# Three quads per gate/up pair, the sums of copies on VectorE, and two-bank transposes in the next pair's last chunks

## The chip, the cores and the metric

The kernel runs on one core of a Trainium2 chip. The metric is device time in microseconds (us) of one execution, as the median over repeated executions. Five engines work from their own in-order instruction streams: TensorE (PE in the profile, with its weight loads as PEld), VectorE (DVE), ScalarE (ACT), GpSimd (POOL), and SyncE (SP), which issues the weight transfers.

## The reference

Two transformer blocks over 256 positions of width 2048, all in float32. The first has three attention branches, the second a gated recurrence, a short convolution and a feed-forward network. The change lies in the feed-forward network alone:

```python
h2 = _rmsnorm(x, ffn_norm_w[l])
g, u = jnp.split(jnp.einsum('bsd,df->bsf', h2, w_gate_up[l]), 2, axis=-1)
x = x + jnp.einsum('bsf,fd->bsd', jax.nn.silu(g) * u, w_down[l])
```

Here `h2` is 256 x 2048, `w_gate_up` is 2048 x 11264 (gate and up, 5632 columns each) and `w_down` is 5632 x 2048.

## The kernel before

**Products in two parts.** A float32 product is made of three matmuls. ScalarE copies a weight tile to a rounded `wh` (`hi`, line 393), VectorE subtracts to get the rest `wl` (`lo`, line 398), and the activations are split the same way. TensorE then multiplies high by high, low by high and high by low. One matmul has 128 x 128 stationary activations and 512 moving columns of weights.

**Pieces.** All products form one list of pieces that `drive` walks through. For each piece it emits the splits of pieces up to five ahead (`feed`, with `la` = 5 and `ahead` = 1 in the feed-forward network), then the matmuls of the piece (`prod`), then what becomes due after it (`done`), and then, for most pieces, one step of the side work (`side`). What `done` and `side` emit for VectorE therefore stands in VectorE's stream behind the splits of the next five pieces. `side` moves the generators in `urgent` and `lanes`. A generator that yields n is taken up again at the n-th later step, and `wait(ev)` asks at each step whether an event was set.

**A chunk** holds two rows of 128 of the contraction for 512 columns: 12 matmuls, one load of 512 KB, one `wh` and one `wl` of 128 x 1024.

**A pair** (`Pair`, line 155) makes the 512 gate columns and the 512 up columns of block j together. For a part of the contraction it goes by quads. A quad (line 285) covers two rows of 128 of the contraction for both 512-column halves and both halves of the positions, and makes this 2 x 2 x 2 block product with seven products instead of eight (Strassen in Winograd's form), so with 21 matmuls instead of 24. In return VectorE makes four sums of weight tiles (`formt`, `formv`, lines 237 to 244) and splits four tiles: g (128 x 1024), u (128 x 512), t and v (128 x 1024 each). The seven products P1 to P7 lie in seven PSUM banks. Before, quads 0 to 3 (`NQ` = 4) cover rows 0 to 7 of the contraction, and rows 8 to 15 go by four chunks of gate (`ga`) and four of up (`gb`). The order of the pieces is quad 0, ga 0, quad 1, ga 1, quad 2, ga 2, quad 3, ga 3, gb 0 to gb 3. Jobs f1 to f10 are such pairs; f0 is made of two plain jobs.

**Sums of copies.** After the last quad ScalarE copies P1, P5, P7 and P6 to SBUF (`ps`, line 274), and the four sums of these copies follow on GpSimd (lines 276 to 282). After gb 0, `evac_a` adds P2 and P4 to two of the sums and applies silu (`sg`, lines 1875 to 1881). After the last gb, `evac_b` adds P3 and Q to the other two (`up`, line 1889) and multiplies (line 1890).

**Transposes.** The finished block j (`sg`, 256 x 512) has to be transposed and split for the down projection (`finish`, lines 1846 to 1862). From f1 on there is one PSUM bank for such side work (bank 7) and seven for products (`wide`, line 1910). `later` makes four transposes into bank 7 at the third step after the block is done, splits them (`ah` on ScalarE, `al` on VectorE) one step later, makes the other four two steps on, and splits those. For most blocks this falls among the quads of the next pair. For blocks 3, 7 and 10 a down projection follows (`fd0`, `fd1`, `fd2`), and it falls among its chunks.

**Storage.** All larger tiles share 43 slots of 128 x 1024, given out in the order in which they came free. The third pair of a group (f3, f7) can hold all 43 by the code: residual 4, `h3` 8, transposed forms 4, `ah`/`al` of three blocks 6, one `sg`, 5 raw loads, t and v, 7 `wh` and 6 `wl`.

Of the kernel before, what the change touches and what calls it, by code (L numbers as in the profile page):

```python
# [13 lines left out]
ALU = mybir.AluOpType  # L14
# [13 lines left out]
RAW = 4  # L28
LA = 3
NSLOT = 43  # L30
NQ = 4
WARM = 4
T2 = 5
RAMP = 6
# [80 lines left out]
class Chunk(Piece):  # L115
# [32 lines left out]
    def done(self, b):  # L148
        b.slots.put(self.wh, self.wl)
        if self.last:  # L150
            self.job.evac([x[:, :self.n] for x in self.job.banks])
            b.free(*self.job.banks)
# [34 lines left out]
class PairChunk(Chunk):  # L187
# [22 lines left out]
    def done(self, b):  # L210
        b.slots.put(self.wh, self.wl)
        if self.last and self.i:
            p = self.job.p
            self.job.evac_b([(p["P3"], p["C12"]), (p["Q"], p["C22"])])
            b.free(p["P3"], p["Q"])
        elif self.then:
            p = self.job.p
            self.job.evac_a([(p["P2"], p["C11"]), (p["P4"], p["C21"])])
            b.free(p["P2"], p["P4"])


class QuadPart(Piece):
# [44 lines left out]
    def done(self, b):  # L267
        b.slots.put(self.wh, self.wl)
        if self.last:
            P_ = self.pair.p  # L270
            for n in self.names:
                if n in ("P1", "P5", "P6", "P7"):
                    P_[n + "s"] = b.work([P, 512], "ps")
                    b.act(P_[n + "s"], P_[n])
                    b.free(P_[n])
            if self.kind == "v":
                p1, p5, p6, p7 = (P_[n + "s"] for n in ("P1", "P5", "P6", "P7"))
                b.tt(p6, p6, p1, ALU.add, "g")
                b.tt(p7, p7, p6, ALU.add, "g")
                b.tt(p6, p6, p5, ALU.add, "g")  # L280
                b.tt(p5, p5, p7, ALU.add, "g")
                P_.update(C11=p1, C12=p6, C21=p7, C22=p5)


def quad(pair, q, first, last):
# [12 lines left out]
class Builder:  # L298
# [1188 lines left out]
    def x_next(self, x, cb, ssp, r, store, g, name):  # L1487
# [5 lines left out]
        def later():  # L1493
            yield 2
            yield from self.gen_T(lambda t, j: x[:, t, j * P:(j + 1) * P], h, l, g=g, ev=f"{name}{cb}")
            for t in range(2):
                sq = self.work([P, 768], "sq", bufs=1)[:, :512]
                self.act(sq, x[:, t, :], AF.Square, accum_out=ssp[:, t, cb:cb + 1])
            if name == "h3" and 2 * cb < NQ:
                yield from self.gen_forms(h, l, cb)  # L1500
# [325 lines left out]
    def ffn(self):  # L1826
        nc, I, sl, jobs = self.nc, self.I, self.slots, self.jobs
        wg, wd = I["w_gate_up"][0], I["w_down"][0]
        k16 = list(range(16))
        h3 = self.h3  # L1830
        xk = lambda k: (h3[k // 4][0][:, k % 4, :], h3[k // 4][1][:, k % 4, :])
        aT, sg = {}, {}
        self.ssf = self.const([P, 2, 4], "ss_f")
        self.gf = []

        def g_evac(j):
            def evac(pts):
                if j == 0:
                    self.force("r_h3")
                s = sl.get([P, 2, 512], F32, "sg")  # L1840
                for t in range(2):
                    self.act(s[:, t, :], pts[t], AF.Silu, scale=self.r3[:, t:t + 1])
                sg[j] = s
            return evac

        def finish(j, s):
            h, l = sl.get([P, 4, 256], F32R, f"ah{j}"), sl.get([P, 4, 256], F32R, f"al{j}")
            aT[j] = (h, l)

            def later():  # L1850
                for b in range(2):
                    yield 2 if b else 3
                    p = self.ps()
                    for jj in range(2):
                        for t in range(2):
                            self.tr(p[:, jj * 256 + t * P:jj * 256 + (t + 1) * P], s[:, t, (2 * b + jj) * P:(2 * b + jj + 1) * P])
                    yield 1
                    fl = lambda a: a[:, 2 * b:2 * b + 2, :].rearrange("p a b -> p (a b)")
                    self.split(fl(h), fl(l), p)
                sl.put(s)  # L1860
                self.done(f"aT{j}")
            self.add(later(), urgent=True)
            if j == 10:
                for v in h3 + list(self.sx.values()):
                    sl.put(*v)

        def u_evac(j):
            def evac(pts):
                s = sg.pop(j)
                for t in range(2):  # L1870
                    self.stt(s[:, t, :], pts[t], self.r3[:, t:t + 1], s[:, t, :], ALU.mult, ALU.mult)
                finish(j, s)
            return evac

        def ga_evac(j):
            def evac(parts):
                s = sg[j] = sl.get([P, 2, 512], F32, "sg")
                for t, (p, q) in enumerate(parts):
                    self.tt(s[:, t, :], p, q, ALU.add)
                for t in range(2):  # L1880
                    self.act(s[:, t, :], s[:, t, :], AF.Silu, scale=self.r3[:, t:t + 1])
            return evac

        def ub_evac(j):
            def evac(parts):
                s = sg.pop(j)
                for t, (p, q) in enumerate(parts):
                    c = self.work([P, 512], "up")
                    self.tt(c, p, q, ALU.add)
                    self.stt(s[:, t, :], c, self.r3[:, t:t + 1], s[:, t, :], ALU.mult, ALU.mult)  # L1890
                finish(j, s)
            return evac

        def d_evac(third, cb):
            def evac(pts):
                x = self.x1[cb]
                if third == 2 and cb == 0:
                    for i in range(2):
                        g = sl.get([P, 1024], F32, f"gf{i}")
                        nc.gpsimd.dma_start(g, I["final_norm_w_2"][i * 1024:(i + 1) * 1024].partition_broadcast(P))  # L1900
                        self.gf.append(g)
                for t in range(2):
                    self.tt(x[:, t, :], pts[t], x[:, t, :], ALU.add)
                if third < 2 and cb == 3:
                    for v in aT.values():
                        sl.put(*v)
                    aT.clear()
            return evac

        def wide():  # L1910

            self.abanks = deque(list(range(4, 7)) + list(self.abanks))
            self.sbanks = deque([7])
            self.nraw, self.la, self.ahead = 5, 5, 1

        ak = lambda k: (aT[k // 4][0][:, k % 4, :], aT[k // 4][1][:, k % 4, :])
        xs = lambda q, i: [v[:, i, q % 2, :] for v in self.sx[q // 2]]
        for third, js in enumerate((range(4), range(4, 8), range(8, 11))):
            for j in js:
                if j == 0:  # L1920
                    jobs.append(Job(f"fg{j}", xk, wg, j * 512, 512, g_evac(j), k16, {2 * c: [f"h3{c}"] for c in range(4)}))
                    jobs.append(Job(f"fu{j}", xk, wg, 5632 + j * 512, 512, u_evac(j), k16))
                else:
                    jobs.append(Pair(f"f{j}", xk, xs, wg, j * 512, 5632 + j * 512, ga_evac(j), ub_evac(j), range(NQ), k16[2 * NQ:],
                                     wide if j == 1 else None))
            ks = list(range(4 * js[0], 4 * js[-1] + (4 if third < 2 else 4 - KG)))
            for cb in range(4):
                jobs.append(Job(f"fd{third}{cb}", ak, wd, cb * 512, 512, d_evac(third, cb), ks,
                                {2 * i: [f"aT{j}"] for i, j in enumerate(js)} if cb == 0 else None))

        for cb in range(4):
            jobs.append(Job(f"fz{cb}", ak, wd, cb * 512, 512, None, list(range(44 - KG, 44))))
# [76 lines left out]
```

## Time and profile before

| | us |
|---|---|
| median of 3 runs (2267.36 to 2269.58) | 2268.35 |
| the profiled execution | 2267.79 |
| its span | 2266.0 |
| f1 to f3, first matmul to the down projection | 141.42 |
| f4 to f7 | 179.65 |
| f8 to f10 | 132.02 |

The profiled execution took 1.8 us more than its span and is within the range of the runs. In the views, the idle time in brackets stands in front of an instruction and names what ended it; a line number is that of the kernel before, and helpers such as line 326 (`tt`) serve many callers, so that the tiles' names tell them apart. Matmuls are pipelined: one of 512 columns is shown with some 0.39 us but follows the one before it every 0.227 us, so stretches and starts are read rather than busy times.

### The profile page before, as it was taken

The page shows a single profiled execution, that of the slowest core. Times are in us where ns is not written, and L with a number is a line of the kernel's source. Part 1 is how long each engine was busy: PE and PEld are TensorE (multiplying, and loading weights), DVE is VectorE, ACT ScalarE, POOL GpSimd, SP SyncE. Part 2 cuts the span into 40 slices and gives each one's busy share as a digit, 9 for nine tenths or more (in the row PEclk, how much of TensorE's full clock was granted, in tenths as well). Part 3 has the DMA queues.
Part 4 walks back from the last instruction along what each step waited for, and adds up shares of the span by engine and source line. Part 5 has one row for each costly group of instructions (what it writes and reads, how often), then busy time and mean ns, then how long its engine had stood idle before and what let it go on. Part 6 is the DMA issues. An engine that isn't in the chain of part 4 may idle for free.

```text
span 2266.0 us, 27833 instructions
## 1 busy us (share of the span) xinstructions
PE 2220.8 (98%) x10396; PEld 1849.9 (82%) x10396; DVE 1556.0 (69%) x1774; ACT 1145.3 (51%) x1532; POOL 402.9 (18%) x284
## 2 busy tenths in 40 slices
PE   9999999999999999999999999999999999999998
PEld 7888888879888888888888888887778877788776
DVE  5675776645756654555786786566996799858984
ACT  5634545455554543353645555453554465535562
POOL 2020103102305011000473351110120011101111
PEclk9999999999999999999999999999999999999999
DMA  9556455545556565656555556554546554565572
GB/s 316 188 180 200 140 167 182 168 144 194 174 158 200 180 184 183 224 185 186 176 161 166 156 155 196 185 193 143 206 165 206 186 204 158 197 202 187 186 253 72
DMA packets 215046, 413.99 MB, mean 183 GB/s; under 512 B 13538, under 2 KB 20432, under 8 KB 214912
## 3 DMA queue, kind: packets, MB, share of 16 engines
q1 hardware_dynamic: 211968, 405.99, 55.8%
q0 software_dynamic: 2224, 5.13, 0.7%
q8 instruction: 81, 1.33, 0.2%
q10 hardware_dynamic: 720, 1.11, 0.1%
q14 instruction: 53, 0.43, 0.1%
HBM read 408.51 MB, written 3.67 MB: 182 GB/s over the span
## 4 chain that ended last, share of the span: by engine, by line
PE 78%; DVE 5%; ACT 2%; issue 1%; POOL 0%; ACTq 0%; DVEq 0%; POOLq 0%
PE acc L143 20%; PE acc L144 20%; PE acc L146 20%; PE sp L351 3%; PE acc L206 2%; PE acc L205 2%; PE acc L208 2%; PE sp L371 2%; DVE wl L398 2%; PE acc L265 2%; PE acc L263 2%; PE acc L264 2%; ACT wh L393 1%; DVE formt L326 1%; DVE formv L326 1%
## 5 line engine op out<-in xcount | busy, mean ns | idle before, releaser
L398 DVE TENSOR_TENSOR wl<-raw,wh 128x1024 fp32r<-128x1024 f32 (+2 forms) x763 | 961.8, 1297 | 319.3 <-ACT wh L393 260.6
L393 ACT ACTIVATE wh<-raw 128x1024 fp32r<-128x1024 f32 (+2 forms) x763 | 742.2, 1025 | 156.9 <-DVE wl L398 88.3
L143 PE MATMUL acc<-wh,xh 128*128 128x512 f32 (+2 forms) x864 | 339.3, 393 | 0.0
L144 PE MATMUL acc<-wh,xl 128*128 128x512 f32 (+2 forms) x864 | 335.5, 388 | 0.0
L146 PE MATMUL acc<-wl,xh 128*128 128x512 f32 (+2 forms) x864 | 229.9, 388 | 0.0
L143 PE MATMUL acc<-wh,h2h 128*128 128x512 f32 x512 | 202.2, 395 | 0.0
L144 PE MATMUL acc<-wh,h2l 128*128 128x512 f32 x512 | 199.4, 390 | 0.0
L146 PEld LDWEIGHTS acc<-wl,xh 128*128 128x128 f32 x864 | 162.2, 188 | 32.7
L144 PEld LDWEIGHTS acc<-wh,xl 128*128 128x128 f32 x864 | 162.4, 188 | 30.9
L143 PEld LDWEIGHTS acc<-wh,xh 128*128 128x128 f32 x864 | 162.4, 188 | 30.7
L326 POOL TENSOR_TENSOR ps<-ps 128x512 f32<-128x512 f32 x40 | 69.6, 1740 | 590.0 <-ACT ps L322 587.7
L143 PE MATMUL acc<-wh,ah 128*128 128x512 f32 x352 | 137.5, 391 | 0.0
L144 PE MATMUL acc<-wh,al 128*128 128x512 f32 x352 | 137.0, 389 | 0.0
L146 PE MATMUL acc<-wl,h2h 128*128 128x512 f32 x512 | 136.9, 389 | 0.0
L205 PE MATMUL acc<-wh,h3h 128*128 128x512 f32 x320 | 124.5, 389 | 0.0
L206 PE MATMUL acc<-wh,h3l 128*128 128x512 f32 x320 | 124.5, 389 | 0.0
L146 PEld LDWEIGHTS acc<-wl,h2h 128*128 128x128 f32 x512 | 96.1, 188 | 20.0
L144 PEld LDWEIGHTS acc<-wh,h2l 128*128 128x128 f32 x512 | 96.3, 188 | 18.9
L143 PEld LDWEIGHTS acc<-wh,h2h 128*128 128x128 f32 x512 | 96.2, 188 | 18.9
L393 ACT ACTIVATE wh<-formt 128x1024 fp32r<-128x1024 f32 x40 | 42.5, 1061 | 134.6 <-DVE formt L326 124.1
L146 PE MATMUL acc<-wl,ah 128*128 128x512 f32 x352 | 94.8, 389 | 0.0
L208 PE MATMUL acc<-wl,h3h 128*128 128x512 f32 x320 | 85.5, 389 | 0.0
(492 smaller groups left out, 3773.4 us busy)
## 6 DMA issues: line engine op xcount, KB each, us to landing
raw<-in_w_in_dram SPq DMA_DIRECT2D x328, 512.0 KB, 3.7
raw<-in_w_gate_up_dram SPq DMA_DIRECT2D x176, 512.0 KB, 4.6
raw<-in_w_down_dram SPq DMA_DIRECT2D x88, 512.0 KB, 4.6
raw<-in_w_out_dram SPq DMA_DIRECT2D x64, 512.0 KB, 3.8
raw<-in_w_branch_dram SPq DMA_DIRECT2D x48, 512.0 KB, 3.9
raw<-in_w_mem_kv_dram SPq DMA_DIRECT2D x31, 512.0 KB, 7.1
raw<-in_w_in_dram SPq DMA_DIRECT2D x8, 464.0 KB, 3.8
raw<-in_w_in_dram SPq DMA_DIRECT2D x8, 448.0 KB, 3.4
```

The lines of the kernel that those rows point to most:

```text
L143: b.nc.tensor.matmul(outs[t], x, self.wh[:, kk], start=self.first and kk == 0, stop=False)
L144: b.nc.tensor.matmul(outs[t], y, self.wh[:, kk], start=False, stop=False)
L146: b.nc.tensor.matmul(outs[t], x, self.wl[:, kk], start=False, stop=self.last and kk == len(self.ks) - 1)
L205: b.nc.tensor.matmul(outs[t], x, self.wh[:, kk], start=self.first and kk == 0 and t == 1, stop=False)
L206: b.nc.tensor.matmul(outs[t], y, self.wh[:, kk], start=False, stop=False)
L208: b.nc.tensor.matmul(outs[t], x, self.wl[:, kk], start=False, stop=self.last and kk == len(self.ks) - 1)
L263: b.nc.tensor.matmul(P_[n], h, self.wh[:, j], start=self.first, stop=False)
L264: b.nc.tensor.matmul(P_[n], l, self.wh[:, j], start=False, stop=False)
L326: (self.nc.vector if eng == "v" else self.nc.gpsimd).tensor_tensor(out, a, b, op=op)
L351: self.nc.tensor.matmul(out, lhsT, rhs, start=start, stop=stop)
L393: self.nc.scalar.activation(wh, src, AF.Copy)
L398: self.nc.vector.tensor_tensor(wl, src, wh.bitcast(F32), op=ALU.subtract)
```

## The change

There are three edits. `NQ` goes from 4 to 3: a pair has three quads, rows 6 to 15 of the contraction go by five ga and five gb chunks, and the order is quad 0, ga 0, quad 1, ga 1, quad 2, ga 2, ga 3, ga 4, gb 0 to gb 4. The four sums of copies leave GpSimd and the end of the last quad; VectorE makes them after gb 0, directly in front of `evac_a`, and there an event named after the pair is set. The transposes of block j wait for the event of pair j+1 (blocks 3, 7 and 10 wait three steps as before). All eight are then made in one step, into bank 7 and one bank taken from the seven, and both halves are split one step later.

```diff
-NQ = 4
+NQ = 3
@@ PairChunk.done
         elif self.then:
             p = self.job.p
+            p1, p5, p6, p7 = (p[n + "s"] for n in ("P1", "P5", "P6", "P7"))
+            b.tt(p6, p6, p1, ALU.add)
+            b.tt(p7, p7, p6, ALU.add)
+            b.tt(p6, p6, p5, ALU.add)
+            b.tt(p5, p5, p7, ALU.add)
+            p.update(C11=p1, C12=p6, C21=p7, C22=p5)
+            b.events.add(self.job.name)
             self.job.evac_a([(p["P2"], p["C11"]), (p["P4"], p["C21"])])
             b.free(p["P2"], p["P4"])
@@ QuadPart.done
-            if self.kind == "v":
-                p1, p5, p6, p7 = (P_[n + "s"] for n in ("P1", "P5", "P6", "P7"))
-                b.tt(p6, p6, p1, ALU.add, "g")
-                b.tt(p7, p7, p6, ALU.add, "g")
-                b.tt(p6, p6, p5, ALU.add, "g")
-                b.tt(p5, p5, p7, ALU.add, "g")
-                P_.update(C11=p1, C12=p6, C21=p7, C22=p5)
@@ finish
             def later():
-                for b in range(2):
-                    yield 2 if b else 3
-                    p = self.ps()
+                if j in (3, 7, 10):
+                    yield 3
+                else:
+                    yield from self.wait(f"f{j + 1}")
+                banks = [self.ps(), self.acc()]
+                for b, p in enumerate(banks):
                     for jj in range(2):
                         for t in range(2):
                             self.tr(p[:, jj * 256 + t * P:jj * 256 + (t + 1) * P], s[:, t, (2 * b + jj) * P:(2 * b + jj + 1) * P])
-                    yield 1
+                yield 1
+                for b, p in enumerate(banks):
                     fl = lambda a: a[:, 2 * b:2 * b + 2, :].rearrange("p a b -> p (a b)")
                     self.split(fl(h), fl(l), p)
+                self.free(banks[1])
                 sl.put(s)
                 self.done(f"aT{j}")
```

## Rows read from the trace of the kernel before

**Rows 1.** The page, part 1: busy us (share of the span) xinstructions.
```profile
PE 2220.8 (98%) x10396; PEld 1849.9 (82%) x10396; DVE 1556.0 (69%) x1774; ACT 1145.3 (51%) x1532; POOL 402.9 (18%) x284
```
**Rows 2.** Busy time by stretch, f1-f3, f4-f7, f8-f10: stretch, length, engines' busy us.
```profile
core 0: us, PE busy (x) PEld busy (x) DVE busy (x) ACT busy (x) POOL busy (x), PEclk, DMA share, GB/s
1560.84:1702.26 141.42, 128.49 (x565) 102.76 (x564) 129.78 (x141) 82.04 (x99) 21.09 (x12) 1.00 0.53 182
1790.26:1969.91 179.65, 170.36 (x746) 137.85 (x744) 168.92 (x183) 103.96 (x126) 27.59 (x16) 0.99 0.55 191
2057.91:2189.93 132.02, 125.96 (x558) 102.47 (x556) 125.32 (x135) 77.35 (x94) 21.48 (x13) 1.00 0.58 201
```
**Rows 3.** The same view, one stretch each for f2 and f4.
```profile
1607.73:1654.60 46.87, 42.83 (x189) 34.26 (x188) 44.09 (x49) 26.19 (x32) 6.72 (x4) 1.00 0.57 191
1790.26:1831.06 40.80, 40.80 (x181) 33.78 (x180) 40.32 (x44) 24.23 (x29) 6.71 (x4) 1.00 0.60 206
```
**Rows 4.** TensorE's waits from f1 to f10: us in total, times, longest.
```profile
PE sp L371 <- DVE al L326: 12.4, 8, 2.1
PE acc L265 <- DVE wl L398: 10.2, 8, 1.7
PE acc L263 <- DVE up L326: 5.2, 10, 0.7
```
**Rows 5.** TensorE in f2, in order: start, us, instruction, [idle before, ended by].
```profile
1611.95 0.47 PE L263 MATMUL acc<-wh,sh 128*128 128x512 f32 x1 [0.66 <-DVE up L326]
...
1616.77 0.60 PE L371 MATMUL sp<-ident,sg 128*128 128x128 f32 x4
1617.12 0.48 PE L263 MATMUL acc<-wh,h3h 128*128 128x512 f32 x1
...
1626.56 0.66 PE L371 MATMUL sp<-ident,sg 128*128 128x128 f32 x4 [1.66 <-DVE al L326]
...
1638.58 0.50 PE L265 MATMUL acc<-wl,sh 128*128 128x512 f32 x1 [1.36 <-DVE wl L398]
```
**Rows 6.** VectorE from the end of f1 to the end of f2, in order.
```profile
1599.94 3.48 DVE L326 TENSOR_TENSOR formt<-raw 128x512 f32<-128x512 f32 x2
1603.34 1.79 DVE L398 TENSOR_TENSOR wl<-raw,wh 128x512 fp32r<-128x512 f32 x1
...
1611.12 0.68 DVE L326 TENSOR_TENSOR up<-acc,ps 128x512 f32<-128x512 f32 x1
...
1615.03 1.29 DVE L326 TENSOR_TENSOR formt<-raw 128x512 f32<-128x512 f32 x2
1616.23 0.69 DVE L398 TENSOR_TENSOR wl<-raw,wh 128x512 fp32r<-128x512 f32 x1
...
1622.85 1.29 DVE L326 TENSOR_TENSOR formt<-raw 128x512 f32<-128x512 f32 x2
...
1625.81 0.69 DVE L326 TENSOR_TENSOR al<-sp,ah 128x512 fp32r<-128x512 f32 x1 [1.07 <-ACT ah L322]
...
1639.72 5.76 DVE L398 TENSOR_TENSOR wl<-raw,wh 128x1024 fp32r<-128x1024 f32 x5
...
1658.06 0.68 DVE L326 TENSOR_TENSOR up<-acc,ps 128x512 f32<-128x512 f32 x1
```
**Rows 7.** GpSimd at the end of f1, in order.
```profile
1599.33 6.95 POOL L326 TENSOR_TENSOR ps<-ps 128x512 f32<-128x512 f32 x4 [69.72 <-ACT ps L322]
```
**Rows 8.** VectorE at the start of f4 and its third quad, in order.
```profile
1790.23 1.29 DVE L326 TENSOR_TENSOR x<-acc,x 128x512 f32<-128x512 f32 x2 [2.12 <-PE acc L146]
...
1803.47 1.22 DVE L398 TENSOR_TENSOR wl<-formt,wh 128x1024 fp32r<-128x1024 f32 x1
```
**Rows 9.** TensorE, first matmul of f1 and first of its first chunk.
```profile
1560.84 0.39 PE L263 MATMUL acc<-wh,h3h 128*128 128x512 f32 x1
...
1567.13 0.39 PE L205 MATMUL acc<-wh,h3h 128*128 128x512 f32 x1
```
**Rows 10.** ScalarE after `evac_a` of f2, in order.
```profile
1652.74 1.34 ACT L322 ACTIVATE sg<-sg,r 128x512 f32<-128x512 f32 x2 [1.30 <-DVE sg L326]
```
**Rows 11.** DMA issues from f1 to f3: xcount, KB each, median us to landing.
```profile
raw<-in_w_gate_up_dram SPq DMA_DIRECT2D x40, 512.0 KB, 4.9
```

## The prediction

> **What bounds the kernel now.** The busy shares come first: TensorE is shown busy for 98% of the span and VectorE for 69% [rows 1]. That average hides the stage of the change, so the next view is busy time by stretch. The ten pairs fill three stretches of 141.42, 179.65 and 132.02 us, 453.09 us together, and in them VectorE is busy for 92 to 95% of the time [rows 2]. One pair shows what TensorE alone would need: f4 takes 40.80 us for its 180 matmuls (four quads of 21, eight chunks of 12), which is 0.2267 us for each, with no pause [rows 3]. Ten such pairs are 408.0 us. The transposes of eight blocks fall into pairs, two groups of four for each block; a group takes 0.35 us (1616.77 to 1617.12) [rows 5], so they are 8 x 0.7 = 5.6 us. The rest, 453.1 - 408.0 - 5.6 = 39.5 us, is TensorE standing still, and it is nearly all that this change can win.
>
> TensorE's waits say for whom: 12.4 us for `al` (the second group of transposes needs bank 7, which VectorE hasn't read yet), 10.2 us for `wl`, 5.2 us for `up` (a bank that `evac_b` has not read) [rows 4]. All three end on VectorE. The order in time shows why: in f2 VectorE works from one `evac_b` (1611.12) to the next (1658.06), 46.94 us, and its only pauses of note are two of 1.07 us in front of `al` [rows 6]. So **in the steady pairs VectorE's stream sets the pace, at 46.9 us, and TensorE, which needs some 41.5, follows.** f4 is the counter-example: it begins with VectorE ahead after a down projection and has no transposes among its quads, and TensorE never waits.
>
> **The change part by part, for a steady pair.**
>
> *Three quads.* TensorE loses 21 matmuls and gains two chunks of 12, so 3 x 0.2267 = +0.68 us per pair, +6.8 us in all. This is certain and has no cover. VectorE loses a quad: from one `formt` to the next is 7.82 us (1615.03 to 1622.85) with one chunk's `wl` in it [rows 6]; a chunk's `wl` is 5.76 / 5 = 1.15 us, so a quad is 6.7 us. It gains two `wl`, 2.3 us. Loads stay 16 per pair.
>
> *Sums on VectorE.* GpSimd's four sums fill 6.95 us from 1599.33 [rows 7]. In that time two `formt` take 3.48 us where they otherwise take 1.29, and a 512-column `wl` takes 1.79 where it otherwise takes 0.69 [rows 6]: VectorE loses 3.3 us. Four sums of the shape of a `formt` (1.29 / 2) cost it 2.6 us. The move is worth 0.7 us to VectorE, if GpSimd is what slows those three. Queued behind the sums are `evac_a`, then the forms and splits of the next pair's t and v; no consumer of `sg` is due before `evac_b`, four chunks later.
>
> The Trainium skill has a rule against this edit: "Perfetto Trace Analysis", section "Optimizing Scalar/DVE Operations", lets work be moved from a saturated VectorE to ScalarE or even GpSimd. The same section adds that the two share an SBUF read port, so such a move might not help. The stretched `formt` in the trace side with the caveat; by the rule without it, the edit costs 2.6 us per pair instead of giving 0.7.
>
> *Transposes in the gb chunks.* The eight follow gb 0 of the next pair. Both pauses of 1.07 us leave the quads, and so do TensorE's 12.4 us, because each group has a bank of its own. VectorE will wait once for the first `ah` behind gb 1. No row shows that place. Below it costs 0; above, ScalarE has the two silu (1.34 us [rows 10]) in front of `ah`, so 1.07 + 1.34 = 2.4 us. I take 1.3, near the row of today. For TensorE I count 0.95 us per block (two groups of 0.35 to 0.40, and 0.2 of refilling). The extra bank was last read by ScalarE in the last quad, long before. Blocks 3, 7 and 10 stay in down projections that have no stall to give back: nothing, within 1 us.
>
> *The sum for VectorE:* 46.9 - 3.3 - 6.7 + 2.3 + 2.6 - 2.1 + 1.3 = **41.0 us**. TensorE needs 183 x 0.2267 + 0.95 = **42.4 us**. TensorE becomes the bound with 1.4 us to spare.
>
> *Is VectorE in time at each place?* In f4 the `wl` of the third quad's t is done at 1804.69, 14.5 us after VectorE turned to the evacuation at the start of the pair [rows 8]. TensorE wants it after two quads, two chunks and 11 matmuls, 77 x 0.2267 = 17.5 us after its start. In a pair behind a pair the evacuation is `evac_b`, 2.77 us (1611.12 to 1613.89, two `up` and two products) instead of 1.2, so 1.4 us of the 3.0 remain. That is enough, but thin: I leave 0.3 us of stall in each of the seven steady pairs (bounds 0 and 1.5). In f1, quad 0 takes 6.29 us [rows 9] where 21 matmuls need 4.76; VectorE can't start the evacuation of f0 sooner, so these 1.5 us stay, and I add 0.8 for quads 1 and 2, which it follows closely.
>
> *What is late next:* the loads. Ten come in a row without a quad to slow their use (ga 2 to gb 4 and two of the next pair), and a load lands 4.9 us after its issue [rows 11]. With five raw tiles ahead this is covered: VectorE ran through five chunks in 5.76 us without a pause [rows 6].
>
> **Sum.** 10 x 41.48 = 414.8, transposes 8 x 0.95 = 7.6, f1 2.3, steady pairs 7 x 0.3 = 2.1: 426.8 us instead of 453.1. The profiled execution of 2267.79 us would become 2241.5. It lies 0.56 us below the median, so I predict **2242 us**. The case's own bounds: no stall but f1's 1.5 and transposes at 0.7 give 421.9 (2237); 1.5 us in each steady pair and 3 in f1 give 435.9 (2251).
>
> **The rivals.**
>
> *A. VectorE stays the bound.* If those three instructions are slowed by something other than GpSimd's sums, or the sums cost VectorE just as much, the 3.3 us remain: its stream is 44.3 us, 1.9 more than TensorE's 42.4, in seven pairs 13 us: **2255**. For it: VectorE's margin is 3% of a pair. Against it: the slow three lie inside GpSimd's 6.95 us, and the same instructions outside are fast. The rule about a saturated VectorE would end here too.
>
> *B. The transposes don't land where meant.* The event is asked for once per step; if it is seen late, the groups slide to the next pair's quads and the two pauses of 1.07 us come back with TensorE's wait, 1.7 us a time [rows 5]: 8 x 1.7 = 14 us, **2256**. Against it: five steps follow the event before the pair ends.
>
> *C. Slower: the slots run out.* `sg` now stays until the next pair's gb 1 instead of its third quad. Where all 43 slots are taken, a new `wh` or raw tile waits for TensorE to finish the piece just before, the lookahead shrinks, and the chain form, copy, `wl` is bare in each quad. One such wait today is 1.36 us [rows 5]; 30 quads make 41 us: 2242 - 2 + 41 = **2281**. It decides from 26.4 / 30 = 0.9 us per quad on. Against it: f3 and f7 can already hold all 43 in their first quads, and the stretch f1 to f3 averages 47.1 us a pair, hardly above f2's 46.87 [rows 2, 3].
>
> **How the numbers follow.** About 0.2% (4.5 us) is what a measurement of this kernel can tell from no change. My case, 2237 to 2251, has 0.67; A 0.16; B 0.04; still faster than 2237, 0.04; C in a mild form that ends within 0.2%, 0.04; C in full, 0.05. So faster 0.91, same 0.04, slower 0.05. The range takes in my case and the nearer half of A and B: 2236 to 2256.
>
> **What would show it.** Right: a steady pair takes 42 to 43 us on TensorE; waits for `al` and `up` are gone from TensorE's list, and those for `wl` shrink to f1; no `formt` is over 0.7 us; VectorE idles before `evac_b`, ended by TensorE; one wait of 1 to 2 us for `ah` per pair. Wrong: VectorE has no idle time before `evac_b` (A), `sp` transposes stand among quads (B), or `wh` copies wait for TensorE's pieces throughout (C). The prediction fails most easily at the 1.4 us margin: 1 us more in VectorE's stream is covered, 3 us are not.

## The result and the profile after

The changed kernel takes 2239.7 us (median of 4 runs, 2238.98 to 2242.56) against 2268.95 us of the kernel before, a ratio of 0.9874 with a 95% interval of 0.9857 to 0.9892: 29 us less. 2242 was predicted.

The page of the changed kernel: the busy line, and the first line of the chain that ended last (shares of the span by engine).

```profile
PE 2222.5 (99%) x10426; PEld 1860.5 (83%) x10426; DVE 1512.5 (68%) x1754; ACT 1129.4 (50%) x1512; POOL 333.3 (15%) x244
...
PE 84%; DVE 1%; ACT 0%; issue 0%; POOL 0%; ACTq 0%; POOLq 0%; DVEq 0%
```

As in [rows 1], the busy shares say little: TensorE goes from 98 to 99%, VectorE from 69 to 68%. The stretches of the pairs say it. The view is busy time by stretch, with the columns of [rows 2]: f1 to f3, f4 to f7, f8 to f10, and f2 alone.

```profile
1564.43:1693.90 129.47, 128.41 (x574) 105.25 (x573) 119.07 (x137) 78.03 (x94) 0.00 (x0) 1.00 0.59 203
1781.84:1950.46 168.62, 168.62 (x757) 139.92 (x756) 153.28 (x177) 97.98 (x118) 0.00 (x0) 1.00 0.60 207
2038.39:2164.63 126.24, 126.24 (x566) 104.73 (x565) 112.96 (x131) 73.59 (x88) 0.62 (x1) 1.00 0.63 214
...
1609.14:1651.52 42.38, 42.38 (x193) 35.19 (x192) 39.28 (x47) 24.50 (x30) 0.00 (x0) 1.00 0.59 203
```

The ten pairs take 424.3 us instead of 453.1 [rows 2], 28.8 less, and this is the whole result: the down projections between them keep their 88 us. TensorE, which had 28 us of idle time shown in these stretches, has 1.1 left, all of it in f1. f2 takes 42.38 us instead of 46.87 [rows 3], and GpSimd does nothing beside it. TensorE's list of waits over the pairs, with three lines in [rows 4], is now this (the second line stood in the list of before too, with the same 0.4 us):

```profile
PE acc L272 <- DVE wl L398: 0.5, 1, 0.5
PE acc L270 <- ACT wh L393: 0.4, 1, 0.4
```

VectorE from one `evac_b` to the next in f2, which answers to [rows 6]:

```profile
1609.12 0.69 DVE L326 TENSOR_TENSOR up<-acc,ps 128x512 f32<-128x512 f32 x1
...
1613.03 1.29 DVE L326 TENSOR_TENSOR formt<-raw 128x512 f32<-128x512 f32 x2
...
1620.85 1.29 DVE L326 TENSOR_TENSOR formt<-raw 128x512 f32<-128x512 f32 x2
...
1633.83 3.50 DVE L398 TENSOR_TENSOR wl<-raw,wh 128x1024 fp32r<-128x1024 f32 x3 [0.21 <-ACT wh L393]
1637.24 2.86 DVE L326 TENSOR_TENSOR ps<-ps 128x512 f32<-128x512 f32 x4
1640.03 1.28 DVE L326 TENSOR_TENSOR sg<-acc,ps 128x512 f32<-128x512 f32 x2
1641.22 1.28 DVE L326 TENSOR_TENSOR formt<-raw 128x512 f32<-128x512 f32 x2
...
1644.18 0.69 DVE L326 TENSOR_TENSOR al<-sp,ah 128x512 fp32r<-128x512 f32 x1 [1.07 <-ACT ah L322]
1644.79 0.68 DVE L326 TENSOR_TENSOR al<-acc,ah 128x512 fp32r<-128x512 f32 x1
...
1651.49 0.69 DVE L326 TENSOR_TENSOR up<-acc,ps 128x512 f32<-128x512 f32 x1 [1.21 <-PE acc L208]
```

The last line carries the result. Before, VectorE came to `evac_b` late, with TensorE waiting. Now it comes 1.21 us early and waits for TensorE's last chunk. Two `formt` take 1.28 or 1.29 us everywhere; over the whole kernel its longest single one is 0.69 us instead of 1.78.

The span fell by 25.4 us, less than the 28.8 of the pairs, because this profiled execution, the longest of the four, reached f1 3.6 us later than that of before: 2.3 us went in the first 15 us and 1.6 near 460 us (0.2 came back between them), in code that the change does not touch. In the later place the granted clock was 0.83 between 455 and 465 us, where the execution of before shows 1.00.

### The profile page after: what moved, and what is told of

It reads as the page before. It is cut to its first block, busy times and chain, and to the rows that moved or that the text cites. A ratio compares the mean times of both kernels' runs of the same rounds, so it can differ in the third digit from the quotient of the medians.

```text
span 2240.6 us, 27730 instructions
## 1 busy us (share of the span) xinstructions
PE 2222.5 (99%) x10426; PEld 1860.5 (83%) x10426; DVE 1512.5 (68%) x1754; ACT 1129.4 (50%) x1512; POOL 333.3 (15%) x244
## 4 chain that ended last, share of the span: by engine, by line
PE 84%; DVE 1%; ACT 0%; issue 0%; POOL 0%; ACTq 0%; POOLq 0%; DVEq 0%
PE acc L143 20%; PE acc L144 20%; PE acc L146 20%; PE acc L206 4%; PE acc L205 4%; PE acc L208 4%; PE sp L351 3%; PE acc L272 2%; PE acc L270 2%; PE acc L271 2%; PE sp L371 2%; PE acc L371 0%; DVE wl L398 0%; ACT x L322 0%; DVE formv L326 0%
## 5 line engine op out<-in xcount | busy, mean ns | idle before, releaser
L205 PE MATMUL acc<-wh,h3h 128*128 128x512 f32 x400 | 156.4, 391 | 0.0
L206 PE MATMUL acc<-wh,h3l 128*128 128x512 f32 x400 | 155.7, 389 | 0.0
L208 PE MATMUL acc<-wl,h3h 128*128 128x512 f32 x400 | 106.9, 389 | 0.0
L208 PEld LDWEIGHTS acc<-wl,h3h 128*128 128x128 f32 x400 | 75.1, 188 | 15.6
```

The costliest lines, as they stand in the source:

```text
L205: b.nc.tensor.matmul(outs[t], x, self.wh[:, kk], start=self.first and kk == 0 and t == 1, stop=False)
L206: b.nc.tensor.matmul(outs[t], y, self.wh[:, kk], start=False, stop=False)
L208: b.nc.tensor.matmul(outs[t], x, self.wl[:, kk], start=False, stop=self.last and kk == len(self.ks) - 1)
```

## The experiments

The theory: in a steady pair VectorE's in-order stream sets the pace as long as it is longer than TensorE's; what shortens that stream counts in full, and nothing counts once TensorE is the longer. The rivals: each of TensorE's waits has its own cause and is cured by its own edit; and, for the sums, VectorE was not slowed by GpSimd at all. The first six runs undo one or two of the three edits, the seventh goes one quad further, the eighth puts the sums back on GpSimd but not at their old place, the next two load GpSimd on purpose, and the last tries to do better. Each experiment's ratio is to runs of the kernel before that were timed beside it (medians of 2268.54 to 2269.51 us). "Pairs" is the sum of the ten pairs, read from the starts of TensorE's matmuls as in [rows 2], and f2 is one steady pair.

| kernel | median us | ratio to before, 95% interval | pairs us | f2 us |
|---|---|---|---|---|
| before | 2268.95 | | 453.1 | 46.87 |
| changed | 2239.70 | 0.9874 [0.9857, 0.9892] | 424.3 | 42.38 |
| e1 quads only | 2242.37 | 0.9883 [0.9870, 0.9897] | 427.6 | 42.51 |
| e2 sums only | 2266.31 | 0.9985 [0.9976, 0.9994] | 449.9 | 46.40 |
| e3 transposes only | 2252.52 | 0.9924 [0.9912, 0.9937] | 436.5 | 45.03 |
| e4 all but quads | 2249.20 | 0.9911 [0.9897, 0.9924] | 432.9 | 44.56 |
| e5 all but sums | 2240.13 | 0.9876 [0.9860, 0.9893] | 424.3 | 42.37 |
| e6 all but transposes | 2243.38 | 0.9888 [0.9873, 0.9903] | 427.0 | 42.47 |
| e7 two quads | 2246.08 | 0.9902 [0.9888, 0.9917] | 430.8 | 43.06 |
| e8 sums behind gb 0, on GpSimd | 2239.11 | 0.9873 [0.9858, 0.9888] | 424.3 | 42.37 |
| e9 extra reads on GpSimd | 2251.60 | 0.9923 [0.9910, 0.9935] | 436.7 | 45.14 |
| e10 extra writes on GpSimd | 2240.10 | 0.9871 [0.9858, 0.9885] | 424.4 | 42.37 |
| e11 better version | 2236.87 | 0.9858 [0.9843, 0.9873] | 420.7 | 42.38 |

Line numbers in the rows below are those of each experiment's kernel.

**e1, three quads alone.**

```diff
-NQ = 4
+NQ = 3
...
```

The rest of the edit sets an event that nothing here waits for.

> The kernel before with three quads alone: sums stay on GpSimd after the last quad, transposes stay where they were. Theory (VectorE's stream sets the pace of a pair, TensorE's when it is longer): VectorE 46.9 - 6.7 + 2.3 = 42.5 us per steady pair, TensorE 42.4, so this edit alone brings nearly all: 2241 to 2247 us. Rival (each wait of TensorE has its own cause, and the 12.4 us for al belong to the single transpose bank): these 12.4 us stay, 2240 + 12 = 2252 us.

Measured: 2242.37 us, 25.5 of the 28.8 us of the pairs. Although the transposes still share one bank, TensorE's waits for `al` in the pairs go from eight of 12.4 us in all to three of 2.5: they went when VectorE was early, without a second bank. The rival's 12 us are not there. VectorE at `evac_b` at the end of f2:

```profile
1649.13 0.69 DVE L327 TENSOR_TENSOR up<-acc,ps 128x512 f32<-128x512 f32 x1 [1.19 <-PE acc L208]
```

Its stream is 42.51 - 1.19 = 41.3 us long, not the 42.5 expected: only one of the two pauses of 1.07 us is left.

**e2, the sums on VectorE alone.**

```diff
-                b.tt(p6, p6, p1, ALU.add, "g")
...
+            b.tt(p6, p6, p1, ALU.add)
...
```

> The kernel before with the sums of copies on VectorE alone (four quads, old transposes). Theory: VectorE's stream gets 3.3 us of slowed instructions back and pays 2.8 for the sums, 0.5 less per steady pair, 7 or 8 pairs: 2264 to 2266 us. Rival (GpSimd is not what slows VectorE; work put on a saturated VectorE costs its full time): 2.8 x 8 = 22 us more, 2290 us.

Measured: 2266.31 us, 3 us less, 0.3 us above the theory's range and far from 2290. VectorE, in order, at the same place where [rows 6] shows 3.48 and 1.79 us:

```profile
1601.41 1.29 DVE L326 TENSOR_TENSOR formt<-raw 128x512 f32<-128x512 f32 x2
1602.61 0.69 DVE L398 TENSOR_TENSOR wl<-raw,wh 128x512 fp32r<-128x512 f32 x1
1603.21 2.87 DVE L326 TENSOR_TENSOR ps<-ps 128x512 f32<-128x512 f32 x4
```

Two `formt` and the `wl` are back at their usual length, 3.3 us less, and the sums cost 2.8. By the rule of "Perfetto Trace Analysis" in the Trainium skill (section "Optimizing Scalar/DVE Operations"), work may move from a saturated VectorE to GpSimd. Here the move the other way gained 0.5 us per steady pair (f2: 46.87 to 46.40). The trace agrees with the section's own caveat that moves between these two, which share a read port, might not help.

**e3, the two-bank transposes alone.**

```diff
-                for b in range(2):
-                    yield 2 if b else 3
-                    p = self.ps()
...
+                if j in (3, 7, 10):
+                    yield 3
+                else:
+                    yield from self.wait(f"f{j + 1}")
+                banks = [self.ps(), self.acc()]
...
```

> The kernel before with the two-bank transposes in the next pair's gb chunks alone. Theory: VectorE's stream loses one of two waits of 1.07 us, 1 us per steady pair: 2260 to 2263 us, although TensorE's 12.4 us of waiting for al are gone; TensorE then waits longer for wl. Rival (each wait has its own cause): all 12.4 us come back, 2256 us.

Measured: 2252.52 us, 16.6 us less in the pairs. Both theories missed: mine gave 6 to 9 us, the rival 12. TensorE's waits over the pairs and VectorE in f1 and f2:

```profile
PE acc L264 <- DVE up L327: 9.2, 10, 1.5
PE acc L266 <- DVE wl L399: 1.2, 3, 0.5
PE acc L264 <- ACT wh L394: 0.4, 1, 0.4
```

```profile
1607.86 0.69 DVE L327 TENSOR_TENSOR al<-sp,ah 128x512 fp32r<-128x512 f32 x1 [0.54 <-ACT ah L323]
...
1611.34 0.69 DVE L327 TENSOR_TENSOR up<-acc,ps 128x512 f32<-128x512 f32 x1
...
1643.58 3.47 DVE L327 TENSOR_TENSOR formt<-raw 128x512 f32<-128x512 f32 x2
```

The waits for `al` are gone, those for `wl` fell from 10.2 to 1.2 us and those for `up` grew from 5.2 to 9.2, though the edit touches neither `wl` nor `up`: as the theory has it, TensorE still waits for a late VectorE, only elsewhere. The size was off, for two reasons. The first is VectorE's pauses for `ah`. In f2 of the kernel before there are two of 1.07 us, the one in [rows 6] and this one:

```profile
1635.38 0.69 DVE L326 TENSOR_TENSOR al<-sp,ah 128x512 fp32r<-128x512 f32 x1 [1.07 <-ACT ah L322]
```

Here there is one of 0.54, not of the 1.1 assumed. That gives 1.6 of the 1.84 us by which f2 got shorter. It is short because of the order of the program. With four quads a pair has one gb chunk less, so `al` stands one piece later in VectorE's stream, behind the `wl` of the next pair's t; ScalarE copies v and then `ah` beside that `wl`. VectorE's line and then ScalarE's:

```profile
1606.11 1.22 DVE L399 TENSOR_TENSOR wl<-formt,wh 128x1024 fp32r<-128x1024 f32 x1
```

```profile
1606.29 1.06 ACT L394 ACTIVATE wh<-formv 128x1024 fp32r<-128x1024 f32 x1 [0.58 <-DVE formv L327]
1607.25 0.58 ACT L323 ACTIVATE ah<-sp 128x512 fp32r<-128x512 f32 x1
```

That VectorE is late is not the reason: in e9 it is late with three quads, and the pause is 1.07 us again. The second reason is f1, f5 and f9, which gain 2.5 us each. In f5 VectorE's stream is 1.7 us shorter (from `evac_b` to `evac_b` 45.11 us instead of 46.81), and VectorE ends the pair 4.18 us behind TensorE where it was 3.38: TensorE, which no longer waits for `al` among the quads, is 0.8 us further ahead. This edit changes the bank and the place of the transposes together; which of the two counts was not tried.

**e4, everything but the quads.**

```diff
-NQ = 3
+NQ = 4
```

> The changed kernel with four quads again. Theory: VectorE 41.2 + 4.4 = 45.6 us per steady pair against TensorE's 41.8, so VectorE is the bound again: 1.3 us less than before's 46.9 in 8 pairs, 2257 to 2260 us. Rival (the waits for al and the sums on GpSimd were the cause, quads only add TensorE work): 6.8 us under the changed kernel, 2233 us.

Measured: 2249.20 us. VectorE is the bound again (TensorE waits 5.8 us for `up`, 2.1 for `wl`), so the rival's 2233 falls. My range was 8 us too high, in part for the first reason of e3: the wait for `ah` is 0.54 us with four quads, and 1.07 was in the 41.2. Also the quad that came back cost VectorE 4.1 us of busy time where 4.4 were assumed. That is 0.8 of the 1.0 us by which f2 stays under the 45.6 expected.

**e5, everything but the sums.** They go back to GpSimd after the last quad.

```diff
+                b.tt(p6, p6, p1, ALU.add, "g")
...
-            b.tt(p6, p6, p1, ALU.add)
...
```

> The changed kernel with the sums back on GpSimd, after the last quad. Theory: VectorE loses 2.8 us of sums and gains up to 3.3 us of slowed instructions, 41.2 + 0.5 = 41.7 us of work and one wait per steady pair, still under TensorE's 42.4: the same time as the changed kernel within 2 us, 2238 to 2242 us. Rival (the move off GpSimd is what made the gain): above 2250 us.

Measured: 2240.13 us, and pairs of 424.3 us, the changed kernel's own. VectorE before `evac_a` of f2:

```profile
1630.49 6.50 DVE L399 TENSOR_TENSOR wl<-raw,wh 128x1024 fp32r<-128x1024 f32 x3 [0.21 <-ACT wh L394]
1636.91 1.27 DVE L327 TENSOR_TENSOR sg<-acc,ps 128x512 f32<-128x512 f32 x2
```

Three `wl` take 6.50 us, 3.0 more than in the changed kernel (3.50), and the 2.86 us of sums are gone: VectorE's stream in f2 is within 0.2 us of the changed kernel's, and with TensorE as the bound the difference is covered anyway. **With three quads the move of the sums is worth nothing.**

**e6, everything but the transposes.**

```diff
-                if j in (3, 7, 10):
...
+                for b in range(2):
+                    yield 2 if b else 3
+                    p = self.ps()
...
```

> The changed kernel with the old transposes (one bank, among the next pair's quads). Theory: VectorE 41.2 + 1.1 = 42.3 us, level with TensorE's 42.4; the second group can still wait for the bank, since al stands in VectorE's stream: 2240 to 2246 us. Rival (the 12.4 us of waits for al belong to the single bank): 2240 + 12 = 2252 us.

Measured: 2243.38 us, 2.7 us more in the pairs. One line of TensorE's waits says where:

```profile
PE sp L371 <- DVE al L326: 2.2, 3, 1.7
```

Three waits are left, 1.71 us in f1, 0.24 in f3 and 0.28 in f7: f1 takes 45.97 us instead of 44.71, f3 and f7 0.5 us more each, the other pairs that hold transposes 0.1.

**e7, two quads.**

```diff
-NQ = 3
+NQ = 2
```

> The changed kernel with two quads per pair. Theory: VectorE is no longer the bound with three, so a further quad less only adds 10 x 3 matmuls of 0.2267 us: 6.8 us more, less up to 1 us from f1's quads: 2245 to 2247 us. Rival (VectorE still sets the pace with three): faster than the changed kernel, under 2238 us.

Measured: 2246.08 us, 6.5 us more in the pairs. VectorE at `evac_b` at the end of f2:

```profile
1649.24 0.69 DVE L326 TENSOR_TENSOR up<-acc,ps 128x512 f32<-128x512 f32 x1 [5.29 <-PE acc L208]
```

VectorE now waits 5.29 us there instead of 1.21 and TensorE pays 0.68 us per pair for matmuls. That is the price of a quad less without its gain.

**e8, the sums in their new place but on GpSimd.**

```diff
-            b.tt(p6, p6, p1, ALU.add)
+            b.tt(p6, p6, p1, ALU.add, "g")
...
```

> The changed kernel with the four sums on GpSimd but in their new place, behind gb 0 (not after the last quad). Theory: GpSimd's 7 us now lie beside the next pair's forms and evac_a waits for two sums (3.5 us), with ScalarE's silu and the split of the transposes behind it: VectorE 41.2 - 2.8 + 3.3 + up to 2 us of waiting = 42 to 44 us per steady pair: 2240 to 2252 us, and formt of over 1.2 us in the trace. Rival (the place of the sums does not matter, only which engine makes them): as with the sums on GpSimd after the last quad.

Measured: 2239.11 us, as e5. The rival was right and my picture wrong: GpSimd, at the end of f2,

```profile
1629.48 8.56 POOL L326 TENSOR_TENSOR ps<-ps 128x512 f32<-128x512 f32 x4 [32.74 <-ACT ps L322]
```

starts as soon as ScalarE's copies are there, not where the program has the sums among other engines' work. They lie beside the `wl` of the chunks, three of which take 6.50 us as in e5; no `formt` is over 0.69 us.

**e9 and e10, work on GpSimd that nobody needs,** after the last quad of each pair of the changed kernel.

```diff
+            if self.kind == "v":
+                z, x = b.work([P, 768], "sq", bufs=1), b.x1[0]
+                b.nc.gpsimd.tensor_tensor(z[:, :512], P_["P6s"], x[:, 0, :], op=ALU.add)
+                for n in range(3):
+                    b.nc.gpsimd.tensor_tensor(z[:, :512], x[:, 0, :], x[:, 1, :], op=ALU.add)
```

> The changed kernel with extra work on GpSimd whose result nobody uses: after the last quad of each pair four sums of 128 x 512 that read two SBUF tiles each. Theory (GpSimd reading SBUF slows VectorE's two-input instructions beside it): VectorE 41.2 + 3.3 = 44.5 us per steady pair against 42.4, some 2 us in 7 or 8 pairs: 2250 to 2258 us, with wl of over 1.8 us beside the sums. Rival (VectorE's slow instructions in the kernel before had another cause): no change, 2240 us, no slow wl.

In e10 the last two lines are instead:

```diff
+                for n in range(6):
+                    b.nc.gpsimd.memset(z, 0.0)
```

> As the run before, but one such sum and then six memsets of 128 x 768 on GpSimd, which only write SBUF. Theory (it is the reading that slows VectorE): 0.8 us more on VectorE for the one sum, covered by its slack of 1.2: 2239 to 2242 us, and wl beside the memsets at 1.15 to 1.3 us. Rival (any GpSimd work on SBUF slows VectorE): wl beside the memsets slowed as beside the sums, 2245 us or more.

Measured: 2251.60 us with the reads, 2240.10 with the writes. VectorE near the end of f2, e9 (the last line is `evac_b`, reached without a pause):

```profile
1633.82 6.49 DVE L403 TENSOR_TENSOR wl<-raw,wh 128x1024 fp32r<-128x1024 f32 x3 [0.20 <-ACT wh L398]
1640.23 3.95 DVE L331 TENSOR_TENSOR ps<-ps 128x512 f32<-128x512 f32 x4
...
1648.26 0.69 DVE L331 TENSOR_TENSOR al<-sp,ah 128x512 fp32r<-128x512 f32 x1 [1.07 <-ACT ah L327]
...
1654.28 0.68 DVE L331 TENSOR_TENSOR up<-acc,ps 128x512 f32<-128x512 f32 x1
```

In e10, GpSimd's line and then VectorE's; the last line is the second and third of the three `wl`:

```profile
1632.15 4.74 POOL L287 MEMSET sq<- 128x768 f32 x6
```

```profile
1631.14 4.30 DVE L403 TENSOR_TENSOR wl<-raw,wh 128x1024 fp32r<-128x1024 f32 x3 [0.21 <-ACT wh L398]
1635.37 2.85 DVE L331 TENSOR_TENSOR ps<-ps 128x512 f32<-128x512 f32 x4
```

```profile
1633.10 2.35 DVE L403 TENSOR_TENSOR wl<-raw,wh 128x1024 fp32r<-128x1024 f32 x2
```

In e9 the three `wl` take 3.0 us more than in the changed kernel and the four sums 1.1 more, 4.1 together. VectorE's slack was 1.21, so f2 should grow by 2.9; it grew by 2.8. In e10 the first `wl` loses 0.8 us beside the one sum; the other two, beside memsets alone, take 2.35 us as anywhere, the sums after them 2.85, and the pairs keep their length. So VectorE is slowed by GpSimd's reading, and it costs time only as far as it exceeds the slack. "SBUF — State Buffer" in the Trainium skill, section "Who interferes with whom", says this: a VectorE instruction with two SBUF inputs contends with a GpSimd instruction that reads SBUF, not with one that only writes. Both runs agree.

**e11, a version meant to be faster.** f4 and f8 get four quads, and the lookahead of five begins with f0's up job.

```diff
-... range(NQ), k16[2 * NQ:],
+... range(4 if j in (4, 8) else NQ), k16[2 * (4 if j in (4, 8) else NQ):],
...
+        def ahead():
+            self.nraw, self.la, self.ahead = 5, 5, 1
...
+                    jobs[-1].begin = ahead
```

> A version meant to be faster: the changed kernel, but f4 and f8, which begin behind a down projection with VectorE ahead, have four quads, and the lookahead of five pieces starts one job earlier (with f0's up job) so that quad 0 of f1 is split in time. Theory: 2 x 0.68 us of matmuls less and up to 2.2 us of f1's stall less: 2236 to 2238 us. Rival (VectorE, 0.9 us late at the end of f4 before, is late again and hands it on): the same as the changed kernel.

Measured: 2236.87 us, inside the expectation. The stretches f1, f4 and f5:

```profile
1560.93:1603.31 42.38, 42.38 (x192) 35.20 (x191) 37.89 (x45) 24.72 (x30) 0.00 (x0) 1.00 0.63 199
1776.01:1816.81 40.80, 40.80 (x182) 33.81 (x181) 40.22 (x48) 24.75 (x30) 0.00 (x0) 1.00 0.61 210
1816.81:1859.19 42.38, 42.38 (x192) 35.20 (x191) 39.65 (x48) 25.20 (x31) 0.00 (x0) 1.00 0.60 199
```

f1 loses its whole stall (44.71 to 42.38), f4 takes 40.80 us instead of 41.48 and hands nothing on to f5. The pairs are 3.7 us shorter than the changed kernel's. The interval of the ratio overlaps with the changed kernel's, and the two were not timed side by side, so the traces show this gain and the times only fit it.

## Why the prediction was right

**The bound and its reversal** held. VectorE's stream was summed to 41.0 us; in f2 it is 42.37 from `evac_b` to `evac_b` less 1.21 of waiting at the end, 41.2. TensorE was given 42.4 with its transposes, and f2 takes 42.38. The slack of 1.4 us is measured as 1.2.

**The terms.** Three quads cost TensorE +0.68 us per pair (f4: 40.80 to 41.48). They save VectorE 4.1 us against 4.4 (e4). The sums cost VectorE 2.8 us against 2.6. The wait for `ah` behind gb 1 is 1.07 against 1.3. f1 takes 44.71 us, where 41.48 + 0.95 + 2.3 = 44.73 was put; its quad 0 takes 1.56 us more than its 21 matmuls need and quads 1 and 2 together 0.7, so the parts agree too. The eight transposes take TensorE 0.9 us with refilling.

**Where it was off by 2.3 us.** The term was the 0.3 us left for stalls in each of seven steady pairs, together with 0.05 too much for each block's transposes: 42.73 predicted for such a pair, 42.37 to 42.39 measured, 7 x 0.35 = 2.5 us. The thin places did not bite.

**Its accounts of the single edits** were less good. That the quads carry most was in the sum (4.4 of 5.9 us), and e1 has 25.5 of 28.8. The 2.1 us of pauses were replaced by a wait of 1.3, which fits a kernel with three quads (1.07). It does not fit one with four, where `al` stands one piece later: e3 shows 0.54. Nor had the account a term for the 0.8 us more that TensorE gains in f1, f5 and f9. So moving the transposes alone brings 16.6 us where that account would give some 7. The gains don't add up either: alone they are 25.5, 16.6 and 3.2 us of the pairs, 45.3 together, of which 28.8 can be had, since TensorE's own work then ends the pair.

**The rivals.** A did not happen. It named two conditions and gave both one price, 13 us. The price belongs to the first alone, that something other than GpSimd's sums slows the three instructions: then 3.3 us of slowing and 2.6 us of sums both lie on VectorE. e2, e9 and e10 show that GpSimd's reading is the cause. e9 shows what such a case costs: it puts 4.1 us of slowing on VectorE beside the sums, and the pairs get 12.3 us longer. Under the second condition, sums as dear as the slowing, the stream is 41.0 + 0.7 = 41.7 us, still under TensorE's 42.4. That is near what happened (2.8 us against 3.3 before and 3.0 in e5), and it costs nothing: e5 takes the same time. B did not happen; all transposes of these blocks stand between two chunks. C did not happen: no pair but f1 shows a wait of TensorE at all. What e6 adds in f3 and f7, where slots are scarcest, is 0.5 us each; whether the slots are its cause was not tried.

## What to carry to other kernels

Find the engine whose in-order stream sets the period of a steady stage, sum that stream with its pauses, and do the same for the engine behind it: the gain ends where the second takes over, and edits that each help alone don't add up beyond that point. A wait list names places, not causes; the waits for the transpose bank went when the late engine's stream got shorter, without a second bank (e1), and when only the transposes were changed, two waits that the edit did not touch changed by 9.0 and 4.0 us (e3). Trading matmuls saved by an algorithm against the vector work that it needs has an optimum, and in this kernel the idle time at one hand-over shows it: TensorE waiting there means too many quads (e4), VectorE waiting 5 us means too few (e7).

## What the runs showed of the hardware

Four float32 sums of 128 x 512 on GpSimd stretch VectorE's two-input instructions beside them by 3.0 us (three `wl`: 3.50 to 6.50 us, e5); the same four sums on VectorE itself cost 2.8 us. Six memsets of 128 x 768 beside VectorE's two-input instructions cost it nothing (two `wl` of 128 x 1024 take 2.35 us, the sums 2.85 against 2.86, e10). So for this operation the move between the two engines is nearly even, which I had not expected to come out so close.
